# Layer 2's shift as rows on TensorE, layer 1's gate summed through scratch, and a new order from keys to turn

## The chip, the cores and the metric

The kernel runs on one core of a Trainium2 chip. A core has four compute engines with instruction streams of their own: TensorE (PE in the profile, its weight loads PEld), VectorE (DVE), ScalarE (ACT) and GpSimd (POOL); a fifth, SyncE (SP), issues most DMA transfers. The metric is the device time of one execution in microseconds, the median of several. Lower is better.

## What is computed

Two layers of a decoder trunk on 256 tokens of width 1024, then a final RMSNorm. Each layer is modulated by a condition vector `c`:

```python
for i in range(DEPTH):
    shift, scale, gate = jnp.split(c @ ada_w[i] + ada_b[i], 3, axis=-1)
    h = rmsnorm(x, norm_g[i]) * (1.0 + scale[:, None, :]) + shift[:, None, :]
    y = nsa_mixer(h, ...) if i % N_MIXERS == 0 else mlstm_mixer(h, ...)
    x = x + gate[:, None, :] * y
return rmsnorm(x, final_g)
```

Layer 1 (`i = 0`) is a sparse attention with 16 heads in 4 groups and three branches (compressed, selected, sliding), whose outputs are summed with sigmoid gates and multiplied by a SiLU gate path before the output projection. Layer 2 (`i = 1`) is a chunkwise mLSTM with 8 heads. The change concerns layer 1 from its keys on, the passage ("turn") from layer 1 to layer 2's first products, and two parts of the modulation: layer 1's `gate` and layer 2's `shift`, each a vector of 1024 that is a product of `c` (1024) with a 1024 x 1024 block of `ada_w`.

## The kernel before

Tokens lie in two blocks of 128 partitions (index `a`). Every weight product is made in three float32r terms: a weight is rounded on ACT (`hi`, line 164), its rest is taken on DVE (`lo`, line 169), and PE multiplies rounded by rounded, rounded by rest and rest by rounded. Weights come as 512 KB pieces through a ring of ten raw buffers, issued by SP (line 86), and go into rings of six `wh` and six `wl` buffers (`RAW`, `WBUF`).

*First phase* (up to about 54 us). Layer 1's modulation, norm and the products for queries and the first keys, streamed by eight blocks of the width.

*Keys, values and gate logits* (`nsa`, 54 to 71 us). `kv_block(kk)` makes, for each of eight blocks of the width, the remaining keys (`gemm_ws`, lines 1610 to 1612), one branch's values and another's values with the gate logits (`gemm_tok`, lines 539 to 541). The queries' evacuation and the position embedding stand between the blocks, in a loop.

*Attention* (71 to about 155 us). A list written out by hand, `ORDER`, names every step, and since the schedule is manual here each engine runs its instructions in that order. Per head pair `n` (0 to 7): `S` scores, `m` masked minima (DVE), `e` exponentials (ACT, line 780), `f` factors (DVE), a scaling of the probabilities (line 794), `T` transposes on PE (line 799), `t` their copies (ACT, line 624), `V` values (line 816). A scaling has two branches of two instructions; `s` puts both on DVE, `p` both on POOL, `q` one on each. Around them stand `hidden`, `gelu` and the `c...` steps (compressed branch), `z`, `zt`, `zo` (gate path), `y` and `Y` (gated output and its parts), `out` (the output projection, line 869), `hi` and `lo` (weights), and the modulation:

- `d:s,n`, `column` (line 852): layer 2's shift (n = 0, 1) and scale (n = 2, 3). The weights lie with the output on partitions, and one DVE pass over 128 x 1024 multiplies by `c` and sums along the row. Sixteen passes, two blocks of 128 outputs for each `s`.
- `gr`, `gc`, `gs`, `ga`: layer 1's gate as rows. `ada_rows` (line 226) multiplies on PE, four partial sums side by side in four column groups of 32; `gc` copies them to SBUF; `gs` (line 859) is a float32 product with a selector matrix that adds the four rows and spreads the sum to 128 partitions; `ga` (line 863) adds it to the bias, which a broadcast on ACT's queue has put into `gate0`.

*Turn* (about 146 to 192 us). `turn` is a hand-written sequence: the last output blocks (`last`), residual and squares (lines 1067, 1068, 1111), the norm's root, scaling, transposes (1125), modulation (1135 on DVE, 1137 on ACT), rounding (1143, 1145) and rest (1149), and layer 2's first products (1158) of `narrow` (272 wide) and `wide` (512 wide) weights.

*Layer 2* follows under the framework's own scheduler, which orders it by its own estimates.

Of the kernel before, what the change touches and what calls it, by code (L numbers as in the profile page):

```python
# [23 lines left out]
class Kernel:  # L24
# [119 lines left out]
    def make_hi(self, m):  # L144
# [7 lines left out]
        if kind == "z":  # L152
            r4 = raw.rearrange("p k j (i d) -> p k j i d", i=2)
            views = [((lambda w, i=i: w.rearrange("p (k i j d) -> p k i j d", k=4, i=2, j=2)[:, :, i]), r4[:, :, :, i]) for i in range(2)]
        elif kind == "q":
# [95 lines left out]
    def setup(self):  # L251
# [16 lines left out]
        self.ones1 = self.T(self.p1, [P, 1])  # L268
        g.memset(self.ones1, 1.0)
# [13 lines left out]
        self.bif = self.T(pc, [P, 16])  # L283
        self.int1 = self.T(pc, [P, 8], I32)
# [24 lines left out]
    def small_loads(self):  # L309
        nc, t = self.nc, self.t  # L310
        self.first_small = [(self.pca[:, 32:89], t["second"])]
        self.small = [(self.bif, t["gate_b"].partition_broadcast(P)), (self.pcb, t["mixer"]), (self.compress, t["compress"])]


    def layer1(self):
# [30 lines left out]
        for kk in range(KC):  # L346
            self.add("s", [P, 816], t["keys"][kk])
# [167 lines left out]
    def embed(self, n, o):  # L515
# [3 lines left out]
        self.nc.vector.tensor_tensor(F.rearrange("p u g s -> p g s u"), self.E[n][:, :, o : 16 + o], pe.unsqueeze(1).unsqueeze(1).to_broadcast([P, 4, 16, 8]), op=OP.add)  # L519
# [23 lines left out]
    def nsa(self, acc):  # L543
# [30 lines left out]
        def kv_block(kk):  # L574

            wh, wl = self.take()
            first, last = kk == 0, kk == KC - 1
            for ch in range(2):
                sl = slice(256 + ch * P, 256 + ch * P + P)
                self.gemm_ws(bk[:, ch * 256 : ch * 256 + 256], wh[:, sl], wl[:, sl], kk, first=(first and ch == 0), last=last)  # L580
            for a in range(2):
                self.gemm_tok(bv[:, a * 256 : a * 256 + 256], wh[:, 0:256], wl[:, 0:256], kk, a, first=(first and a == 0), last=last)
            for a in range(2):
                self.gemm_tok(bg[a][:, 0:304], wh[:, 512:816], wl[:, 512:816], kk, a, first=first, last=last)


        bk, bg, bv = self.bank(7), [self.bank(4), self.bank(5)], self.bank(6)
        for kk in range(KC):
            kv_block(kk)
            if kk % 2:  # L590
                self.embed(kk // 2 % 2, kk // 4)
            else:
                queries(kk // 2)
            if kk < 6:
                self.split_next()
        self.dup_split((KH, KL), 1, bk)
        for a in range(2):
            nc.scalar.activation(V[1][:, a], bg[a][:, 0:256], AF.Copy)
            nc.scalar.activation(G[:, a], bg[a][:, 256:304], AF.Tanh, scale=0.5)
        nc.vector.tensor_scalar(G, G, 1.0, 0.25, op0=OP.add, op1=OP.mult)  # L600
# [5 lines left out]
    T:0,0,1 m:1,0 gelu:2 p:0,1 params lo z:0,1 e:1,0 turned t:0,0,1 m:1,1 T:0,0,0 t:0,0,0 S:2,0 second e:1,1 T:0,1,1 cvalues:0 T:0,1,0 f:1 t:0,1,0  # L606
    z:0,2 z:0,3 ckeys cscores:0 cscores:1 hi cvalues:1 zt:0 t:0,1,1 m:2,0 q:1,0 S:2,1 ccopy:0 ccopy:1 d:0,1 T:1,0,1 zo:0 ctokens:0 t:1,0,1 m:2,1
    T:1,0,0 p:1,1 cdist:0 ctokens:1 t:1,0,0 cdist:1 z:1,0 e:2,1 z:1,1 bias cexp T:1,1,1 T:1,1,0 lo e:2,0 cprobs f:2 t:1,1,1 cparts:0 z:1,2 cparts:1 t:1,1,0
    S:3,0 z:1,3 S:3,1 zt:1 m:3,0 m:3,1 d:0,2 q:2,0 cturned:0 V:0 V:1 zo:1 e:3,0 p:2,1 cpt:0 T:2,0,0 e:3,1 C:0 f:3 d:0,3 cturned:1 t:2,0,0 s:3,0
    T:2,0,1 d:1,0 T:2,1,0 cpt:1 t:2,1,0 t:2,0,1 hi gr:0 S:4,0 T:2,1,1 y:0 gc:0 m:4,0 gs:0 ga:0 t:2,1,1 T:3,0,0 hi t:3,0,0 p:3,1 lo S:4,1 T:3,0,1 e:4,0  # L610
    t:3,0,1 m:4,1 S:5,0 e:4,1 z:2,0 T:3,1,1 t:3,1,1 T:3,1,0 z:2,1 hi S:5,1 m:5,0 lo f:4 z:2,2 d:1,1 gr:1 m:5,1 p:4,0 t:3,1,0 e:5,1 p:4,1 d:1,2 z:2,3
    hi T:4,0,0 e:5,0 S:6,0 zt:2 V:2 V:3 lo d:1,3 C:1 lo zo:2 t:4,0,0 gc:1 T:4,1,0 t:4,1,0 T:4,0,1 f:5 s:5,0 y:1 t:4,0,1 S:6,1 T:5,0,0 T:4,1,1 d:2,0
    t:5,0,0 m:6,0 p:5,1 t:4,1,1 gs:1 e:6,0 m:6,1 T:5,0,1 t:5,0,1 e:6,1 d:2,1 V:4 d:2,2 S:7,0 f:6 T:5,1,0 p:6,1 z:3,0 T:5,1,1 m:7,0 t:5,1,0 q:6,0 z:3,1
    ga:1 hi S:7,1 T:6,0,0 z:3,2 Y:0 lo hi z:3,3 C:2 m:7,1 t:5,1,1 out:0 V:5 hi lo T:6,0,1 d:2,3 e:7,1 zt:3 d:3,0 e:7,0 t:6,0,0 zo:3 f:7 hi T:6,1,0
    q:7,0 hi out:1 t:6,1,0 t:6,0,1 d:3,1 T:6,1,1 hi lo y:2 Y:1 t:6,1,1 lo root q:7,1 lo V:6 lo Y:2 d:3,2 d:3,3
    """

    def attention(self, hidden_block):
# [171 lines left out]
        def scaled(n, j, *es):  # L790
            for br in range(2):
                for a in range(2):
                    v = probs(n, j, br, a)
                    es[br].tensor_scalar(v, v, F[n][:, a, br, j : j + 1], None, op0=OP.mult)  # L794
# [59 lines left out]
        def gate_bias():  # L854
            nc.scalar.dma_start(self.gate0, t["ada_b"][0:1, 2048:3072].partition_broadcast(P))

        def gate_sum(bank):
            b = B["gs"] = self.bank(bank)
# [836 lines left out]
```

## Time and profile before

| | us |
|---|---|
| median of three runs | 423.44 (423.31 to 423.47) |
| the profiled execution's own time | 423.31 |
| its span, first to last instruction | 421.5 |
| PE busy / DVE busy / ACT busy / POOL busy | 412.3 / 348.6 / 270.8 / 96.6 |

The granted TensorE clock is 0.996 of full speed over the span. A time in the profile counts from the span's start. "Idle before, releaser" in a row is how long the engine stood still before the instruction, and what it waited for last. Matmuls overlap: a record lasts longer than the distance from its start to the next one's, so a stretch in which PE is busy all the time can still hold late starts; the distance between starts shows them.

### The profile page before, as it was taken

To read this page: it belongs to the slowest core of one execution; us is meant where nothing else is said; L and a number is where in the kernel's file an instruction comes from. 1 tells how busy PE (TensorE), PEld (TensorE's weight loads), DVE (VectorE), ACT (ScalarE), POOL (GpSimd) and SP (SyncE) were. 2 spreads that over 40 slices of the span, in tenths; PEclk is the share of its full clock that TensorE was granted. 3 is DMA by queue.
4 is the path that set the end of the run, shared out by engine and by line. 5 is a ranking of instruction groups with operands and counts; after the bars stand their busy time and mean duration, and the time that the engine had idled before them with its cause. 6 is when DMAs were issued, how large, how long until landed. Compare 5 with 4: busy or idle time off the path is not lost.

```text
span 421.5 us, 7600 instructions
## 1 busy us (share of the span) xinstructions
PE 412.3 (98%) x2669; PEld 357.2 (85%) x2669; DVE 348.6 (83%) x736; ACT 270.8 (64%) x541; POOL 96.6 (23%) x154
## 2 busy tenths in 40 slices
PE   8999999999999999999999999999999999999994
PEld 5899999789778877878999999888888888888884
DVE  6999898999999998878592699899858998558554
ACT  6666693788987973668547966565456554565523
POOL 4000112354676750142223200000000240320000
PEclk9999999999999999999999999999999999999998
DMA  8999996963799678239667467467456587640002
GB/s 321 410 407 406 396 322 197 342 274 136 253 334 388 236 251 298 96 119 317 218 226 277 157 193 225 177 205 265 169 176 202 186 296 230 180 143 0 0 2 100
DMA packets 27543, 96.21 MB, mean 228 GB/s; under 512 B 3512, under 2 KB 3616, under 8 KB 27376
## 3 DMA queue, kind: packets, MB, share of 16 engines
q1 hardware_dynamic: 26208, 92.30, 61.9%
q0 software_dynamic: 1008, 2.63, 1.7%
q10 hardware_dynamic: 288, 0.79, 0.5%
q8 instruction: 21, 0.34, 0.3%
q14 instruction: 18, 0.15, 0.1%
HBM read 94.61 MB, written 1.09 MB: 227 GB/s over the span
## 4 chain that ended last, share of the span: by engine, by line
PE 84%; issue 5%; DMA 4%; POOL 2%; DVE 2%; ACT 1%; SPq 0%; DVEq 0%; POOLq 0%
PE bank L539 10%; PE bank L541 10%; PE bank L540 10%; PE bank L433 7%; PE bank L1612 6%; PE bank L1610 6%; PE bank L1611 6%; PE bank L1523 5%; PE bank L1036 5%; PE bank L1158 3%; DMA Q<-in_columns 3%; PE bank L799 2%; PE bank L1403 2%; PE bank L816 2%; PE bank L754 2%
## 5 line engine op out<-in xcount | busy, mean ns | idle before, releaser
L169 DVE TENSOR_TENSOR wl<-raw,wh 128x1024 fp32r<-128x1024 f32 (+4 forms) x127 | 139.3, 1112 | 34.5 <-ACT wh L164 33.8
L164 ACT ACTIVATE wh<-raw 128x1024 fp32r<-128x1024 f32 (+4 forms) x127 | 119.2, 957 | 65.1 <-PE bank L541 28.2
L539 PE MATMUL bank<-wh,one 128*128 128x512 f32 (+1 forms) x208 | 76.9, 370 | 0.0
L540 PE MATMUL bank<-wl,one 128*128 128x512 f32 (+1 forms) x208 | 76.3, 367 | 0.0
L541 PE MATMUL bank<-wh,one 128*128 128x512 f32 (+1 forms) x208 | 76.2, 367 | 0.0
L1610 PE MATMUL bank<-one,wh 128*128 128x256 f32 x208 | 59.6, 287 | 0.0
L1612 PE MATMUL bank<-one,wl 128*128 128x256 f32 x208 | 59.0, 284 | 0.1
L1611 PE MATMUL bank<-one,wh 128*128 128x256 f32 x208 | 58.8, 283 | 0.0
L794 POOL TENSOR_SCALAR Pr<-Pr,f 128x128 f32<-128x128 f32 (+1 forms) x42 | 46.7, 1128 | 32.9 <-DVE f L788 18.8
L539 PEld LDWEIGHTS bank<-wh,one 128*128 128x128 f32 x208 | 39.2, 188 | 6.2 <-DVE tz L511 0.2
L541 PEld LDWEIGHTS bank<-wh,one 128*128 128x128 f32 x208 | 39.2, 188 | 6.2
L540 PEld LDWEIGHTS bank<-wl,one 128*128 128x128 f32 x208 | 39.2, 189 | 6.0
L1610 PEld LDWEIGHTS bank<-one,wh 128*128 128x128 f32 x208 | 39.7, 191 | 1.4 <-issue 0.8
L1612 PEld LDWEIGHTS bank<-one,wl 128*128 128x128 f32 x208 | 39.7, 191 | 0.5 <-DVE wl L169 0.3
L1611 PEld LDWEIGHTS bank<-one,wh 128*128 128x128 f32 x208 | 39.8, 191 | 0.1
L780 ACT ACTIVATE Pr<-Pr,mn 128x128 f32<-128x128 f32 (+1 forms) x64 | 28.2, 444 | 4.3 <-DVE mn L773 4.3
L433 PE MATMUL bank<-one,wh 128*128 128x256 f32 x224 | 29.8, 284 | 0.5 <-ACT one L407 0.4
L433 PEld LDWEIGHTS bank<-one,wh 128*128 128x128 f32 x224 | 28.1, 192 | 0.9 <-ACT one L407 0.6
L160 POOL TENSOR_TENSOR raw<-raw,gate 128x256 f32<-128x256 f32 x16 | 13.6, 858 | 49.7 <-DMA raw<-in_out_b 24.9
L1384 DVE SCALAR_TENSOR_TENSOR conv<-bank,one,conv 128x255 f32<-128x255 f32 (+2 forms) x48 | 20.0, 466 | 2.1 <-ACT conv L1379 2.1
L852 DVE CUSTOM_DVE_ANT_0 raw<-raw,one,one 128x1024 f32<-128x1024 f32 x16 | 21.1, 1330 | 0.0
L773 DVE CUSTOM_DVE_ANT_0 Pr<-bank,one 128x128 f32<-128x128 f32 (+1 forms) x64 | 18.7, 348 | 0.0
(336 smaller groups left out, 793.1 us busy)
## 6 DMA issues: line engine op xcount, KB each, us to landing
raw<-in_wide SPq DMA_DIRECT2D x44, 512.0 KB, 4.4
raw<-in_units SPq DMA_DIRECT2D x18, 512.0 KB, 4.6
raw<-in_turn SPq DMA_DIRECT2D x16, 512.0 KB, 6.8
raw<-in_gates SPq DMA_DIRECT2D x16, 512.0 KB, 4.9
raw<-in_out_b SPq DMA_DIRECT2D x16, 512.0 KB, 3.9
raw<-in_start SPq DMA_DIRECT2D x8, 512.0 KB, 9.7
Q<-in_columns SPq DMA_DIRECT2D x8, 512.0 KB, 9.6
raw<-in_hidden SPq DMA_DIRECT2D x8, 512.0 KB, 4.3
```

Source lines behind the costliest of these rows:

```text
L164: self.nc.scalar.activation(v(hi), src, AF.Copy)
L169: self.nc.vector.tensor_sub(v(lo), src, v(hi).bitcast(F32))
L433: nc.tensor.matmul(out, w[:, ch * P : ch * P + P], h[:, kk], start=(kk == 0 and m == 0 and ch % 2 == 0), stop=(kk == 7 and m == 2), skip_g ...
L539: nc.tensor.matmul(out, self.hh[:, kk, sl], wh, start=first, stop=False, skip_group_check=True)
L540: nc.tensor.matmul(out, self.hh[:, kk, sl], wl, start=False, stop=False, skip_group_check=True)
L541: nc.tensor.matmul(out, self.hl[:, kk, sl], wh, start=False, stop=last, skip_group_check=True)
L780: nc.scalar.activation(v, v, AF.Exp, bias=mn[:, a, br, j : j + 1], scale=-1.0, accum_out=sm[:, a, br, j : j + 1])
L794: es[br].tensor_scalar(v, v, F[n][:, a, br, j : j + 1], None, op0=OP.mult)
L852: nc.vector.tensor_tensor_reduce(raw, raw, self.cbc, scale, self.pca[:, 72 + 8 * b + kc : 73 + 8 * b + kc], OP.mult, OP.add, self.cols1[s] ...
L1610: nc.tensor.matmul(out, wh, self.hh[:, kk], start=first, stop=False, skip_group_check=skip)
L1611: nc.tensor.matmul(out, wh, self.hl[:, kk], start=False, stop=False, skip_group_check=skip)
L1612: nc.tensor.matmul(out, wl, self.hh[:, kk], start=False, stop=last, skip_group_check=skip)
```

## The change

1. Layer 2's shift is made like the gate: `cr` (rows on PE by `ada_rows`, two groups), `cc` (permuted copy on ACT), `c1` (a store of the four partial rows to DRAM scratch by a POOL DMA), `c2` (a load with outputs spread over 128 partitions), `c3` (a transpose of 32 x 32 blocks, a sum over the four parts and the bias, on DVE). The eight `d:s,0` and `d:s,1` passes are gone, and `modulate` takes the shift from `self.shifts`. The weights come as eight pieces of `shift` instead of eight of `turn`.
2. Layer 1's gate is summed through scratch: `g1` stores the four rows, `g2` loads them as 32 partitions, `g3` adds them and the bias (`gbias`) on DVE, `g4` stores the sum, `g5` loads it broadcast to 128 partitions into `gate0`. The selector product and the addition are gone.
3. The keys loop and the turn are taken apart into steps, and `ORDER` is written anew over all of it, from the keys to the turn. Keys have three parts, `k:kk,part`; scalings are `s` with an engine for each branch (`v` DVE, `p` POOL, `a` ACT), so ACT makes some too.
4. The gate path's weights come in the order that PE reads, so that `hi` and `lo` are one instruction for 1024 columns instead of two strided ones for 512.

```diff
-        nc.scalar.activation(V[0].rearrange("p a k -> p (a k)"), bv, AF.Copy)
-        self.attention(hidden)
+        self.attention({"hidden": hidden, "k": kv_block, "qa": queries, "qb": query_rests, "kd": keys_out, "G": gates_out, "vo": values_out,
+                        "E": lambda n, o: self.embed(n, o, nc.vector), "Ea": lambda n, o: self.embed(n, o, nc.scalar)})
...
-    d:0,0 hidden:0 hi hidden:1 S:0,0 lo S:0,1 hi hidden:2 hidden:3 z:0,0 m:0,0 m:0,1 e:0,0 lo S:1,0 e:0,1 f:0 gelu:0 s:0,0 hi S:1,1 gelu:1
...
+    hi k:0,0 k:0,1 hi lo lo k:0,2 k:1,0 k:1,1 E:1,0 k:1,2 k:2,1 E:0,0 k:3,1 k:2,2 k:2,0 hi hi hi lo E:0,1 k:4,1 qa:2 E:1,1 qa:0 k:3,2 hi qa:1 k:3,0
+    k:4,2 lo k:5,2 k:4,0 k:5,1 qa:3 lo qb:3 qb:2 k:5,0 k:6,2 k:6,0 lo k:7,0 qb:1 hi lo hi hi k:7,2 G:0 qb:0 kd lo G:1 hidden:0 vo:1 hidden:1 S:0,0
+    k:6,1 S:0,1 m:0,0 hi e:0,0 hidden:2 vo:0 lo m:0,1 e:0,1 f:0 hidden:3 sap:0,0 S:1,0 k:7,1 gelu:0 m:1,0 gelu:1 vo:2 S:1,1 m:1,1 T:0,0,0 z:0,0
...
+    t:5,1,0 c1:0 T:5,1,1 t:5,1,1 m:7,0 e:7,0 g3 c1:1 g4 hi z:3,2 z:3,3 T:6,1,1 T:6,1,0 m:7,1 e:7,1 lo lo zt:3 out:0 d:3,2 out:1 l:1,1,2 f:7 t:6,1,1
+    svp:7,1 hi spv:7,0 t:6,1,0 T:6,0,1 t:6,0,1 T:6,0,0 lo lo lo g5 hi t:6,0,0 C:2 zo:3 V:5 l:0,0,2 T:7,1,1 l:0,0,3 y:2 lo hi T:7,1,0 l:0,1,2 t:7,1,1
+    t:7,1,0 T:7,0,1 T:7,0,0 t:7,0,0 V:6 lo t:7,0,1 V:7 c2 C:3 l:0,1,3 Y:2 l:0,1,4 l:0,1,5 l:0,0,4 l:0,0,5 nh:1 nl:1 y:3 c3 Y:3 nh:0 l:0,0,6 nl:0 d:3,3
+    l:0,0,7 r:0,0 l:0,1,6 l:0,1,7 l:1,0,2 r:0,1 root sq:0,0 nh:2 sq:0,1 l:1,1,3 l:1,0,3 l:1,1,4 l:1,0,4 nl:2 sc:0 x:0,1 l:1,0,5 l:1,0,6 l:1,0,7 nh:3
+    nl:3 x:0,0 tr:0,0 tr:0,1 nh:4 rp:1,0 md:0,1 l:1,1,5 l:1,1,6 md:0,0 ro:0,0 l:1,1,7 r:1,1 ro:0,1 n:0,0 n:0,1 sq:1,0 v:0,0 sq:1,1 re:0,0 re:0,1 sc:1
+    x:1,1 nh:5 nl:4 v:0,1 n:0,2 v:1,0 v:1,1 x:1,0 tr:1,0 md:1,0 tr:1,1 md:1,1 v:2,0 v:2,1 ro:1,0 ro:1,1 re:1,1 re:1,0 nl:5 v:0,2 v:1,2 n:1,0 n:1,1
+    n:1,2 gt:0 gt:1
...
-        def gate_sum(bank):
-            b = B["gs"] = self.bank(bank)
-            nc.tensor.matmul(b, self.sel, W["A"].pop(0), start=True, stop=True)
-
-        def gate_add(n):
-            g = self.gate0[:, 512 * n : 512 * n + 512]
-            nc.vector.tensor_tensor(g, g, B["gs"], op=OP.add)
+        def four(A):
+            return A.rearrange("(j r) k -> j r k", r=32)[:, 0]
+
+        def gate_store(n):
+            if not n:
+                W["quarters"] = self.pd.tile([4, D], F32, name=self.nm("quarters"), tag="quarters")
+            nc.gpsimd.dma_start(W["quarters"][:, 512 * n : 512 * n + 512], four(W["A"].pop(("gate", n))))
+
+        def gate_load():
+            W["gq"] = T([32, 4, 32])
+            nc.gpsimd.dma_start(W["gq"], W["quarters"].rearrange("j (b c) -> b j c", b=32))
+
+        def gate_sum():
+            W["gv"] = T([32, 32])
+            nc.vector.tensor_reduce(W["gv"], W["gq"].rearrange("b j c -> b c j"), axis=AX.X, op=OP.add)
+            nc.vector.tensor_tensor(W["gv"], W["gv"], self.gbias, op=OP.add)
...
+        def gate_spread():
+            nc.gpsimd.dma_start(self.gate0, W["whole"].rearrange("b c -> (b c)").unsqueeze(0).partition_broadcast(P))
+
+        def shift_store(n):
+            if not n:
+                W["drawer"] = self.pd.tile([4, 2, 16, 32], F32, name=self.nm("shifts"), tag="shifts")
+            nc.gpsimd.dma_start(W["drawer"][:, n].rearrange("q (j k) c -> j q (k c)", j=4), four(W["A"].pop(("shift", n))).rearrange("j (q k) -> j q k", q=4))
+
+        def shift_load():
+            W["sq"], W["st"] = T([P, 32]), T([P, 32])
+            nc.gpsimd.dma_start(W["sq"], W["drawer"].rearrange("q n r c -> (q n r) c"))
+
+        def shift_sum():
+            sh = self.shifts = self.T(pc, [P, 8])
+            nc.vector.transpose(W["st"], W["sq"])
+            nc.vector.tensor_reduce(sh.rearrange("p (n k) -> p n k", n=2), W["st"].rearrange("p (n j k) -> p n k j", n=2, j=4), axis=AX.X, op=OP.add)
+            nc.vector.tensor_tensor(sh, sh, self.pca[:, 72:80], op=OP.add)
```

In the new steps of the turn, `l:a,half,k` is one output block, `r` and `rp` are the residual with its addition on DVE or POOL, `sq` the squares, `sc` the root, `x` the scaling, `tr` the transposes, `md` the modulation, `ro` the rounding, `re` its rest, `n` and `v` the narrow and wide products, `nh` and `nl` the weights' `hi` and `lo`, `gt` the gate logits.

More of the change, by code (lines that the diff above doesn't have):

```diff
@@ L151, in make_hi @@
         kind = self.queue[m][0]
[L152 to L155, printed above, removed]
+        if kind == "q":
             cuts = (slice(0, 2), slice(2, 4)) if m in self.opening else (slice(0, 4),)
@@ L612 @@
[L612 to L615, printed above, removed]
+        kw, banks = [], {}
@@ new lines, in kv_block @@
+        def kv_block(kk, part):
+            while len(kw) <= kk:
+                kw.append(self.take())
+            if not kk:
+                banks[part] = [self.bank(i) for i in ((7,), (6,), (4, 5))[part]]
+            wh, wl = kw[kk]
+            first, last = kk == 0, kk == KC - 1
+            if part == 0:
+                for ch in range(2):
+                    sl = slice(256 + ch * P, 256 + ch * P + P)
+                    self.gemm_ws(banks[0][0][:, ch * 256 : ch * 256 + 256], wh[:, sl], wl[:, sl], kk, first=(first and ch == 0), last=last)
+            elif part == 1:
+                for a in range(2):
+                    self.gemm_tok(banks[1][0][:, a * 256 : a * 256 + 256], wh[:, 0:256], wl[:, 0:256], kk, a, first=(first and a == 0), last=last)
+            else:
+                for a in range(2):
+                    self.gemm_tok(banks[2][a][:, 0:304], wh[:, 512:816], wl[:, 512:816], kk, a, first=first, last=last)
@@ L1107, in square, with narrow_hi, narrow_lo, last @@
+        def narrow_hi(n):
+            half_made[n] = self.make_hi(self.first + n)
+        def narrow_lo(n):
+            self.make_lo(*half_made.pop(n))
+            self._load()
+        def last(a, half, k):
+            while len(held) < k - 1:
+                n = len(held) + 2
+                held[n] = self.take(hold=n > 2)
+            self.out_mm(k, *held[k], a, *self.pieces[a][half])
         def square(a, half):
-            self.residual(p1, self.gate0, a, *pieces[a][half], g=nc.gpsimd if (a, half) in ((1, 0),) else nc.vector)
@@ L1159, in products @@
                                          stop=(k0 + k == KC - 1 and m == 2), skip_group_check=True)
-        held[2] = self.take()
-        for n in range(4):
-            self.step("T", 7, n // 2, n % 2)
-            self.step("t", 7, n // 2, n % 2)
-            if n < 2:
-                self.split_next()
-            last(n % 2, n // 2, [2])
-        for k in range(3, 8):
-            held[k] = self.take(hold=True)
-        hi(2)
-        self.step("V", 7)
-        self.step("C", 3)
-        hi(0)
@@ L1190, in turn @@
-        for half in range(2):
-            last(1, half, [3])
-        for half in range(2):
-            last(1, half, [4, 5])
-        scale(0)
-        hi(3)
-        lo(3)
-        transposed(0)
-        for half in range(2):
-            last(1, half, [6, 7])
-        modulate(0)
-        hi(4)
-        rounded(0)
-        square(1, 0)
-        rest(0, 0)
-        square(1, 1)
-        rest(0, 1)
-        first = [(3 * n, self.take(hold=n > 0)) for n in range(3)]
-        bs = [self.bank(6 + a) for a in range(2)]
@@ L1223, in turn, with narrow @@
-        rest(1, 0)
-        rest(1, 1)
-        lo(5)
-        w.append((4, self.take(hold=True)))
-        products(vs[0], w[2:], 0, 512, (0, 1))
-        products(bs[1][:, 0:272], first, 1, 272)
-        GT = self.T(pc, [P, 2, 16])
-        for a in range(2):
-            nc.vector.tensor_tensor(GT[:, a], bs[a][:, 256:272], self.bif, op=OP.add)
+        def narrow(a, m):
+            if not first:
+                first.extend((3 * n, self.take(hold=n > 0)) for n in range(3))
+            if not m:
+                bs[a] = self.bank(6 + a)
+            products(bs[a][:, 0:272], first, a, 272, (m,))
@@ L1233, in todo, with wide, gates @@
+        def wide(m, n):
+            if not vs:
+                vs.update((a, self.bank(4 + a)) for a in range(2))
+            while len(w) <= n:
+                w.append((2 * len(w), self.take(hold=True)))
+            products(vs[0], w[n : n + 1], 0, 512, (m,))
+        def gates(a):
+            if "t" not in half_made:
+                half_made["t"] = self.T(pc, [P, 2, 16])
+            nc.vector.tensor_tensor(half_made["t"][:, a], bs[a][:, 256:272], self.bif, op=OP.add)
         def todo():
```

281 lines of the change are left out of this document (120 added, 161 removed).

## The prediction

> **What bounds the kernel now.** I read the page's first table first, then the busy time by stretches, then the steps between TensorE's starts.
>
> ```profile
> PE 412.3 (98%) x2669; PEld 357.2 (85%) x2669; DVE 348.6 (83%) x736; ACT 270.8 (64%) x541; POOL 96.6 (23%) x154
> ```
> ```profile
> 72.00:120.00 48.00, 48.00 (x406) 39.21 (x404) 45.44 (x172) 40.28 (x130) 21.94 (x27) 1.00 0.68 256
> 120.00:155.00 35.00, 34.79 (x265) 27.62 (x258) 34.72 (x94) 29.93 (x82) 26.46 (x22) 1.00 0.82 286
> 155.00:192.00 37.00, 36.18 (x194) 29.22 (x193) 31.03 (x57) 22.01 (x40) 7.25 (x22) 1.00 0.56 195
> 192.00:416.00 224.00, 224.00 (x1269) 196.53 (x1268) 171.65 (x307) 130.26 (x211) 29.01 (x41) 1.00 0.54 180
> ```
>
> The columns after the stretch are its length, then busy time of PE, PEld, DVE, ACT and POOL. Two engines look full in the attention (72 to 155 us): PE 82.8 us of 83 and DVE 45.44 + 34.72 = 80.2 us. Which is the bound? A busy PE may be overlap of modelled ends, so I look at where matmuls start. Of a gate-path run in the timeline:
>
> ```profile
> 87.69 0.28 PE L1611 MATMUL bank<-one,wh 128*128 128x256 f32 x1
> ...
> 90.32 0.28 PE L1612 MATMUL bank<-one,wl 128*128 128x256 f32 x1
> ```
>
> Between these two rows lie 22 steps: 2.63 / 22 = 0.120 us from start to start. A record lasts 0.28 us, so each overlaps the next by 0.16. 512-wide products, in a stretch of the chain of waits where PE waits for nothing, step by 6.91 / 30 = 0.23 us, and so they do in the attention:
>
> ```profile
> 350.88 6.91 PE bank L1036 x30
> ```
>
> So TensorE is dense at its own rate, and DVE, though nearly full, keeps up. What TensorE loses to waits from 54 us to 192 us is little:
>
> ```profile
> PE bank L1158 <- DVE one L1145: 0.5, 1, 0.5
> PE bank L816 <- DVE y L825: 0.2, 1, 0.2
> PE bank L1158 <- DVE one L1149: 0.2, 1, 0.2
> ```
>
> Idle after a record's end costs that idle and the lost overlap of 0.16: 0.49 + 0.16 = 0.65, 0.21 + 0.16 = 0.37 and 0.20 + 0.16 = 0.36 us. In the timeline the second one ends here, the third and the first stand with their surroundings:
>
> ```profile
> 149.63 1.52 PE L816 MATMUL bank<-PT,one 128*64 128x256 f32 x16 [0.21 <-DVE y L825]
> ```
> ```profile
> 176.38 1.68 PE L1158 MATMUL bank<-wh,one 128*128 128x272 f32 x8 [0.20 <-DVE one L1149]
> ...
> 178.37 1.04 PE L1125 MATMUL bank<-one,Pr 128*128 128x128 f32 x8
> ...
> 179.44 1.36 DVE L1135 TENSOR_SCALAR tz<-bank,cols 128x128 f32<-128x128 f32 x4 [0.51 <-PE bank L1125]
> ...
> 180.73 0.41 DVE L1145 CAST one<-tz 128x512 fp32r<-128x512 f32 x1
> ...
> 181.29 0.97 PE L1158 MATMUL bank<-wh,one 128*128 128x272 f32 x5 [0.49 <-DVE one L1145]
> ```
>
> After the second token block's transposes (L1125) PE has too few products to cover the modulation (1.36) and the rounding (0.41) on DVE. These three are 1.4 us. Smaller ones, estimated from starts that come 0.1 to 0.3 us late beside their neighbours (at 55, 57.8, 172 and 186 us), make about 1.2 more. So about 2.6 us is all that a better order can win before 192 us, and from 192 to 416 us PE is busy in every microsecond and waits for nothing. The first 54 us and the tail behind 416 us run code that stays.
>
> **The change part by part.** *TensorE.* The shift as rows adds two groups like layer 1's gate rows; summing the gate through scratch removes the two selector products. From the chain of waits:
>
> ```profile
> 107.97 1.85 PE bank L226 x16
> ...
> 110.82 0.98 PE bank L859 x2
> ...
> 119.72 1.85 PE bank L226 x16
> ...
> 129.66 0.86 PE bank L859 x2
> ```
>
> Added 2 x 1.85 = 3.70, removed 0.98 + 0.86 = 1.84, net +1.86 us on the engine that sets the end. Everything else on PE (keys, hidden, scores, turns, gate path, products) is the same work in another order.
>
> *DVE.* It loses half of L852's sixteen column passes, the two gate sums and two of its 22 scalings (the gate path's weight rests, one wide instruction now instead of two strided ones, give back a little more, which I leave out):
>
> ```profile
> L852 DVE CUSTOM_DVE_ANT_0 raw<-raw,one,one 128x1024 f32<-128x1024 f32 x16 | 21.1, 1330 | 0.0
> ...
> L794 DVE TENSOR_SCALAR Pr<-Pr,f 128x256 f32<-128x256 f32 x11 | 4.4, 400 | 0.0
> L794 DVE TENSOR_SCALAR Pr<-Pr,f 128x128 f32<-128x128 f32 x11 | 3.9, 356 | 0.1
> ...
> L863 DVE TENSOR_TENSOR gate<-gate,bank 128x512 f32<-128x512 f32 x2 | 1.4, 676 | 0.0
> ```
>
> 8 x 1.33 + 2 x 0.676 + (0.400 + 0.356) = 12.7 us less. New are five small sums and a turn of at most 128x32. No row has them; they lie between 0.41 (L1145, 128x512) and nothing, and I take 0.3 each, 1.5 us, keeping 0 to 2.1. DVE is freed of some 11.2 us. Since PE does not wait for DVE in 72 to 149 us, this by itself is worth nothing; its worth is that the order can be drawn tighter.
>
> *ACT.* Counted in the new order, 16 scalings come over from POOL and DVE, and two permuted copies of shift rows; the gate path's 16 half-width roundings become 8:
>
> ```profile
> L780 ACT ACTIVATE Pr<-Pr,mn 128x256 f32<-128x256 f32 x32 | 15.8, 498 | 3.2 <-DVE mn L773 3.2
> ...
> L780 ACT ACTIVATE Pr<-Pr,mn 128x128 f32<-128x128 f32 x32 | 12.4, 390 | 1.1 <-DVE mn L773 1.1
> ...
> L164 ACT ACTIVATE wh<-raw 128x512 fp32r<-128x512 f32 x16 | 9.1, 628 | 0.0
> ...
> L164 ACT ACTIVATE wh<-raw 128x1024 fp32r<-128x1024 f32 x8 | 8.3, 1056 | 0.0
> ...
> L624 ACT ACTIVATE adaA<-bank 128x512 f32<-128x512 f32 x2 | 1.2, 587 | 0.1
> ```
>
> 8 x (0.498 + 0.390) + 2 x 0.587 - (16 x 0.628 - 8 x 1.056) = 7.1 + 1.2 - 1.6 = 6.7 us more, against 83 - 40.28 - 29.93 = 12.8 us that ACT idles in the attention. It fits, with 6.1 us over; at nothing, then, and the second rival is what it costs if that cover is gone.
>
> *POOL and scratch.* POOL's scalings go from 42 to 28, and eight DMA issues are put on its queue: two stores, load, store and spread for the gate, two stores and a load for the shift. Nearest rows:
>
> ```profile
> 213.12 1.95 POOL L1353 DMA_DIRECT2D one<-store  x4
> ```
> ```profile
> DT<-shelf POOLq DMA_DIRECT2D x1, 1536.0 KB, 9.7
> ...
> gate<-in_ada_b ACTq DMA_DIRECT2D x1, 512.0 KB, 4.5
> ...
> QK<-drawer POOLq DMA_DIRECT2D x4, 4.0 KB, 4.9
> ```
>
> An issue takes 1.95 / 4 = 0.49 us, together 3.9, less than the 14 scalings gone. The landing counts only where it ends late. The gate's spread (512 KB to 128 partitions) is issued behind POOL's last scalings and must be there at the first residual. In the new order PE has between the two the value products 5, 6 and 7 (L816, 1.52 us each by the row above) and ten output blocks of three 0.23 us products (0.70), 11.6 us, with some turns and two compressed products besides: about 13 us. By the broadcast rows it takes 4.5 (same size) to 9.7 us (three times the size), and POOL, with a last pair of scalings ahead, may be 2 us late: it fits, at nothing. The shift's load is issued right behind it and its sum stands on DVE behind the last gated product, some 9 us on (the three value products, six of the blocks); 4.9 us fits too. Queued behind that sum on DVE are the last head group's rest (L829) and the residuals, so lateness there would reach PE after some 3 us more of products.
>
> *Queues.* SP issues the same bytes: eight 512 KB pieces of shift rows for eight of columns. ACT's queue loses the bias broadcast. Both at nothing.
>
> *Keys.* The key, value and gate-logit products are cut in three parts per block and two are held back as filler between the first scores; the products are the same and steps of 0.12 to 0.14 us go on across parts. Worth only the late start at 57.8 us: 0.2 us gained, between 0 and 0.3.
>
> *Turn.* Followed by hand with the durations quoted, the new order puts four 512-wide pieces (two steps of 0.23 for each of two blocks) behind the second transposes instead of three, and every rest in time. The 0.36 at 176 us goes, of the 0.65 at 180 us about 0.55 goes; the start at 172 us stays, since there are only three output blocks (2.1 us) ahead where there were four. The wait at 149.6 us goes as values 7 stand right behind values 6. Together 0.36 + 0.55 + 0.37 = 1.3; with the keys 1.5 us.
>
> **Sum**: +1.86 - 1.5 = +0.36; for new waits in the attention I leave nothing, between -0.5 (small late starts vanish) and +1.1 (eleven more of 0.1 us). On the profiled execution's 423.31 us (span 421.5 and 1.8 around it) that is 423.67, and the median before, 423.44, lies 0.13 above that execution. I say **423.6**, with its own range 422.8 to 424.8: no change by what a measurement here can tell (0.2%, 0.85 us).
>
> **The rivals.** *All waits go* (faster): 2.6 us won against 1.86 paid, and the small gaps at switches halved, another 0.5: 423.31 + 1.86 - 3.1 = 422.1 us. For it: DVE's 11.2 us of freed time lies where every one of those waits comes from. Against it: the waits at 55 and 186 us come from code that stays.
>
> *ACT becomes the late engine* (slower). Its idle time is mostly waits that come with the chain itself:
>
> ```profile
> ACT PT L624 <- PE bank L799: 4.5, 6, 1.7
> ACT Pr L780 <- DVE mn L773: 4.3, 5, 1.5
> ```
>
> If these 8.8 us stay, ACT needs 70.2 + 6.7 + 8.8 = 85.7 us in a stage of 83, and its turned copies (L624) hold the banks that PE turns into: 2.7 us late, 426.3; half of it, 425.0. It decides where more than 6.1 us of them remain. DVE being freer speaks against it, as nearly half of them wait for DVE.
>
> *A round trip ends late* (slower): 9.7 us for the spread and 4.9 for the shift's load behind it on the same queue are 14.6 us where 9 are covered up to DVE's sum and 3 more by products behind it: 2.6 us late, 426.2. Landings of more than 12 us together decide it; the 4.5 of the same-size broadcast speaks against.
>
> *DVE is the bound after all* (faster). Then 11.2 us less on DVE would shorten the stage by as much: 423.31 - 11.2 = 412.1 us. The quoted steps of 0.12 us speak against it, and PE's waits for DVE of 0.9 us in all. The Trainium skill (Perfetto Trace Analysis, Identifying the Most-Contended Engine) holds matmul busy time for a bad measure and would judge TensorE's headroom by its weight loads. By that rule PE has room here, as PEld is busy 39.21 of 48 us, and DVE with 45.44 is the most contended engine; the starts in the trace show no such room.
>
> That the shift's rows do not do what they say (columns still made) would show as sixteen L852 passes; the order has eight such steps, so I give it nothing.
>
> **How the numbers follow.** Forecast 0.60, all waits go 0.17, ACT late 0.14, round trip late 0.06, DVE the bound 0.03. Faster by over 0.2% (below 422.6): the two faster rivals, 0.20. Slower by over 0.2% (above 424.3): the two slower ones and the top of the forecast's own range, 0.14 + 0.06 + 0.05 = 0.25. Same: 0.55. The range 422.0 to 425.2 takes in the forecast with its bounds, the first rival and ACT's up to a half.
>
> **What would show it.** Right: 64 records of L226's kind with 128x512 where there were 32 and none of the selector products; steps of 0.12 and 0.23 us as now; DVE busy some 11 us less; PE's waits on DVE at the second rounding near 0.1 us. Wrong: PE waiting for ACT's turned copies or scalings (second rival), for the first residual's gate or a DVE sum behind a DMA (third), or a stage from 72 to 155 us that has shrunk by more than 3 us (fourth).

## The result, and the profile after

The changed kernel takes 428.25 us (427.98 to 428.67, four runs) against 423.46 us (423.31 to 424.23, four runs) for the kernel before on the same chip: ratio 1.0112, 95% interval 1.0097 to 1.0127. It is 1.1% slower. The forecast was 423.6 us, and the time lies above the range of 422.0 to 425.2.

The first table of the page after, and the busy time by the same stretches as before (length, then busy time of PE, PEld, DVE, ACT and POOL):

```profile
PE 416.2 (98%) x2697; PEld 359.1 (84%) x2697; DVE 336.9 (79%) x713; ACT 276.1 (65%) x551; POOL 85.0 (20%) x148
```
```profile
72.00:120.00 48.00, 47.21 (x405) 38.58 (x402) 37.71 (x143) 39.78 (x131) 14.01 (x20) 1.00 0.63 225
120.00:155.00 35.00, 34.23 (x263) 27.05 (x263) 31.11 (x98) 27.93 (x80) 18.82 (x22) 1.00 0.86 337
155.00:192.00 37.00, 36.92 (x215) 30.45 (x215) 29.68 (x58) 23.66 (x44) 6.32 (x21) 1.00 0.53 174
192.00:416.00 224.00, 224.00 (x1240) 194.01 (x1239) 169.99 (x300) 130.69 (x209) 33.55 (x44) 1.00 0.55 180
```

DVE lost 11.7 us of busy time and ACT gained 5.3, about as counted (11.2 and 6.7). In the attention PE now has small holes (47.21 of 48 us and 34.23 of 35, where it was 48.00 and 34.79), in the turn fewer (36.92 of 37, where it was 36.18). The last row is the surprise: from 192 to 416 us PE is busy all the time, as before, but gets through 1240 products instead of 1269. A part of that is only the later start of this stretch, so the next cut is made at products and not at times.

Where along the span did the time come? I took the starts of three products that both kernels have: the last of the first phase, the last of the turn (the rows of lines 1158 before and 1192 after), and the last one of all (line 1523 before, 1510 after). Of the kernel before:

```profile
L1158 PE MATMUL bank<-wl,one x32: 284/340/482, 173.6 to 192.0; 128*128 128x272 f32 x16, 128*128 128x512 f32 x16
```
```profile
415.76 0.28 PE L1523 MATMUL bank<-late,V 128*128 128x256 f32 x1
```

and of the changed one:

```profile
L1192 PE MATMUL bank<-wl,one x32: 284/342/480, 176.2 to 193.8; 128*128 128x272 f32 x16, 128*128 128x512 f32 x16
```
```profile
420.37 0.28 PE L1510 MATMUL bank<-late,V 128*128 128x256 f32 x1
```

| stretch of TensorE | before | after | difference | predicted |
|---|---|---|---|---|
| up to the last first-phase product | 52.26 | 52.57 | +0.31 | 0 |
| from there to the last product of the turn | 139.79 | 141.24 | +1.45 | +0.36 |
| from there to the last product | 223.72 | 226.55 | +2.83 | 0 |

The largest part lies in a stretch whose code did not change, in which both kernels run 1268 products and PE waits for nothing. So the products themselves must be slower. The source rows of the second of `gemm_tok`'s three products (`tok_unit` calls it all through layer 2), 208 records, before (line 540) and after (541), with the shortest, median and longest duration in ns:

```profile
L540 PE MATMUL bank<-wl,one x208: 280/389/400, 53.2 to 392.4; 128*128 128x512 f32 x80, 128*128 128x256 f32 x16, 128*128 128x304 f32 x8
```
```profile
L541 PE MATMUL bank<-wl,one x208: 277/395/401, 53.5 to 397.0; 128*128 128x512 f32 x80, 128*128 128x256 f32 x16, 128*128 128x304 f32 x8
```

The same products last 395 ns instead of 389. Start to start, in the timeline near 200 us, before:

```profile
199.75 0.39 PE L540 MATMUL bank<-wl,one 128*128 128x512 f32 x1
...
202.69 0.39 PE L541 MATMUL bank<-wh,one 128*128 128x512 f32 x1
```

and after:

```profile
199.44 0.39 PE L540 MATMUL bank<-wh,one 128*128 128x512 f32 x1
...
204.82 0.39 PE L542 MATMUL bank<-wh,one 128*128 128x512 f32 x1
```

Before, 13 steps in 2.94 us are 0.226 each; after, 23 steps in 5.38 us are 0.234. Over the 480-odd 512-wide products of this kind the mean rose from 227.9 to 234.1 ns: 480 x 6.2 ns = 3.0 us, enough for the whole of the +2.83. The granted clock is 1.00 in this stretch in both.

In the middle stretch the waits changed places. PE's waits after, from the view of waits:

```profile
PE bank L776 <- POOL KL L534: 0.8, 1, 0.8
PE bank L821 <- POOL Pr L816: 0.8, 2, 0.6
```

Gone are the waits for DVE that ended at 149.6, 176.4 and 181.3 us (of the last a late start of 0.17 us is left) and two smaller late starts at 57.8 and 172.5 us. New are two for POOL. The timeline of POOL shows what it did before the second one:

```profile
115.72 0.57 POOL L884 DMA_DIRECT2D quarters<-adaA  x1 [1.83 <-ACT adaA L643]
121.12 0.58 POOL L888 DMA_DIRECT2D one<-quarters  x1 [4.83 <-DVE wl L166]
121.74 4.62 POOL L816 TENSOR_SCALAR Pr<-Pr,f 128x128 f32<-128x128 f32 x6
```

`g2`, the load of the four quarters, reads what `g1` has just stored. It stood 4.83 us at the head of POOL's queue, and the scalings of head pair 3 stood behind it. The releaser that the row names (a `wl` on DVE) has nothing to do with this load; the store's landing fits, and a later run names it.

### The profile page after: what moved, and what is told of

It is laid out like the page before. It is cut to its first block, busy times and chain, and to the rows that moved or that the text cites. A ratio compares the mean times of both kernels' runs of the same rounds, so it can differ in the third digit from the quotient of the medians.

```text
span 426.2 us, 7639 instructions
## 1 busy us (share of the span) xinstructions
PE 416.2 (98%) x2697; PEld 359.1 (84%) x2697; DVE 336.9 (79%) x713; ACT 276.1 (65%) x551; POOL 85.0 (20%) x148
## 4 chain that ended last, share of the span: by engine, by line
PE 86%; DVE 4%; DMA 3%; ACT 2%; issue 1%; SPq 1%; POOL 1%; DVEq 0%; ACTq 0%
PE bank L541 9%; PE bank L542 9%; PE bank L540 9%; PE bank L430 8%; PE bank L921 5%; PE bank L1510 5%; PE bank L1081 5%; PE bank L1597 5%; PE bank L1599 5%; PE bank L1598 5%; PE bank L1192 4%; PE bank L838 3%; DMA raw<-in_start 2%; PE bank L821 2%; PE bank L1390 2%; PE bank L773 2%
## 5 line engine op out<-in xcount | busy, mean ns | idle before, releaser
L540 PE MATMUL bank<-wh,one 128*128 128x512 f32 (+2 forms) x208 | 77.9, 375 | 0.0
L541 PE MATMUL bank<-wl,one 128*128 128x512 f32 (+2 forms) x208 | 77.3, 372 | 0.0
L542 PE MATMUL bank<-wh,one 128*128 128x512 f32 (+2 forms) x208 | 77.1, 372 | 0.0
L1598 PEld LDWEIGHTS bank<-one,wh 128*128 128x128 f32 x208 | 39.4, 189 | 0.1
L1597 PEld LDWEIGHTS bank<-one,wh 128*128 128x128 f32 x208 | 39.1, 188 | 0.1
L816 POOL TENSOR_SCALAR Pr<-Pr,f 128x128 f32<-128x128 f32 (+1 forms) x28 | 25.5, 925 | 24.6 <-DVE f L807 15.3
L430 PEld LDWEIGHTS bank<-one,wh 128*128 128x128 f32 x224 | 28.0, 189 | 1.1 <-ACT one L404 0.6
L157 POOL TENSOR_TENSOR raw<-raw,gate 128x256 f32<-128x256 f32 x16 | 16.3, 1028 | 48.2 <-DMA raw<-in_out_b 24.6
L643 ACT ACTIVATE PT<-bank 128x384 f32<-128x384 f32 x32 | 14.9, 486 | 8.3 <-PE bank L821 8.3
```

The costliest lines, as they stand in the source:

```text
L430: nc.tensor.matmul(out, w[:, ch * P : ch * P + P], h[:, kk], start=(kk == 0 and m == 0 and ch % 2 == 0), stop=(kk == 7 and m == 2), skip_g ...
L540: nc.tensor.matmul(out, self.hh[:, kk, sl], wh, start=first, stop=False, skip_group_check=True)
L541: nc.tensor.matmul(out, self.hh[:, kk, sl], wl, start=False, stop=False, skip_group_check=True)
L542: nc.tensor.matmul(out, self.hl[:, kk, sl], wh, start=False, stop=last, skip_group_check=True)
L816: es[br].tensor_scalar(v, v, f, None, op0=OP.mult)
L1597: nc.tensor.matmul(out, wh, self.hh[:, kk], start=first, stop=False, skip_group_check=skip)
```

## The experiments

Two theories. **Placement**: two small tiles of the change (`gbias`, 128 bytes a partition, and `shifts`, 32) lie ahead of the weight rings in SBUF (the on-chip memory that holds all tiles, each at its address in the partitions) and push them on by 160 bytes, while `hh` and `hl`, the other operand of these products, stay; dense products are slower for it. **Queue**: the new waits of the attention come from steps that POOL or DVE holds at the head of its queue for a landing. The rival to the first is that the new order or its traffic (scratch, streams) slows layer 2.

**1. a_home**: the changed kernel, its order untouched, with the two tiles where they do not move the rings.

```diff
-        self.gbias = self.T(pc, [32, 32])
+        self.gbias = self.T(self.p1, [32, 32])
+        self.shifts = self.T(self.p1, [P, 8])
...
-            sh = self.shifts = self.T(pc, [P, 8])
+            sh = self.shifts
```

> The changed kernel with its two new small tiles (gate bias, 128 bytes per partition, and shifts, 32) taken from the layer 1 pool instead of the constant pool; every instruction and its order stay. The weight rings then begin at byte 41088 as before (0 modulo 64) and not at 41248 (32 modulo 64). Theory 'place of the rings': the 480 products of 512 columns in layer 2 that stream weights against the norm's rows step by 0.227 to 0.230 us again instead of 0.234 to 0.236; layer 2 gets 2.9 us back; time 425.3. Rival 'layer 2's neighbours' (another order or another timing of DVE, ACT and DMA beside the products): the steps stay at 0.234 and the time at 428.2.

Measured: 425.28 us (424.3 to 425.76, ten runs) against 423.96, ratio 1.0027, interval 1.0017 to 1.0038. Its source row of the same product:

```profile
L542 PE MATMUL bank<-wl,one x208: 278/389/400, 53.2 to 393.3; 128*128 128x512 f32 x80, 128*128 128x256 f32 x16, 128*128 128x304 f32 x8
```

389 ns again, and 223.70 us from the turn to the end, as before. Placement is shown, and three quarters of the loss with it (1.12% to 0.27%).

**2 and 3. b_pad32, b_pad64**: the kernel before with an unused tile ahead of the rings.

```diff
         self.bif = self.T(pc, [P, 16])
+        self.T(pc, [P, 8])        # b_pad32; [P, 16] in b_pad64
```

> The kernel before with 32 unused bytes per partition in the constant pool, so that the weight rings begin at 32 modulo 64; nothing else. Place of the rings: 512-wide steps of 0.234 us in layer 2, 426.3 us. Layer 2's neighbours: 423.4, since no instruction moves.

> The kernel before with 64 unused bytes: the rings keep 0 modulo 64 and move by 64 modulo 128. If the place counts modulo 64: steps of 0.227 to 0.230 us and 423.4. If it counts modulo 128 or more: steps up to 0.234 us and up to 426.3. Layer 2's neighbours: 423.4.

Measured: with 32 bytes 425.38 us (424.89 to 426.37) against 423.96, ratio 1.0036, interval 1.0026 to 1.0046; the 512-wide step is 233.2 ns. So an unused tile alone, with no change of code, slows the kernel by half as much as was expected. Half, because the 256-wide products, whose stationary operand is the weight, became faster at the same time: 119.7 to 118.2 ns. With 64 bytes the single run gave 422.24 us, less than the kernel before: 512-wide 229.6, but 256-wide 116.5 ns. Of this gain 0.89 us was there at the end of the first phase already (51.37 us against 52.26 in the trace of the kernel before), and from the turn to the end it takes 223.65 us, hardly less than before. A rule by the place within 64 bytes gives neither the 229.6 nor the 116.5.

**4. b_gate**: the kernel before with only the gate through scratch, its steps at the places of the old ones and its bias tile in layer 1's pool, where it does not move the rings. Two of the changed lines of `ORDER`:

```diff
-    T:2,0,1 d:1,0 T:2,1,0 cpt:1 t:2,1,0 t:2,0,1 hi gr:0 S:4,0 T:2,1,1 y:0 gc:0 m:4,0 gs:0 ga:0 t:2,1,1 T:3,0,0 hi t:3,0,0 p:3,1 lo S:4,1 T:3,0,1 e:4,0
+    T:2,0,1 d:1,0 T:2,1,0 cpt:1 t:2,1,0 t:2,0,1 hi gr:0 S:4,0 T:2,1,1 y:0 gc:0 m:4,0 g1:0 t:2,1,1 T:3,0,0 hi t:3,0,0 p:3,1 lo S:4,1 T:3,0,1 e:4,0
...
-    ga:1 hi S:7,1 T:6,0,0 z:3,2 Y:0 lo hi z:3,3 C:2 m:7,1 t:5,1,1 out:0 V:5 hi lo T:6,0,1 d:2,3 e:7,1 zt:3 d:3,0 e:7,0 t:6,0,0 zo:3 f:7 hi T:6,1,0
+    g3 g4 hi S:7,1 T:6,0,0 z:3,2 Y:0 lo hi z:3,3 C:2 m:7,1 t:5,1,1 out:0 V:5 hi lo T:6,0,1 d:2,3 e:7,1 zt:3 d:3,0 e:7,0 t:6,0,0 zo:3 f:7 hi T:6,1,0
```

> The kernel before with one part of the change alone: layer 1's gate summed through scratch (two stores, load, sum with the bias on DVE, store, spread), put into the old order at the places of the old steps, the spread behind POOL's last scaling. Rings at their old place. If TensorE's work sets the time, the two selector products (0.98 + 0.86 us) go and nothing comes: 421.6. If a round trip ends late, PE waits before the first residual or a DVE sum: 423.4 or more.

Measured: 428.33 us (428.16 to 428.67), ratio 1.0100, interval 1.0083 to 1.0116. The expectation of 421.6 was missed by 6.7 us, though the two selector products are gone. The timeline of DVE shows one of the two places, that of POOL the other:

```profile
142.46 0.36 DVE L866 TENSOR_REDUCE one<-adaA 32x32 f32<-32x128 f32 x1 [4.45 <-DMA adaA<-quarters]
```
```profile
111.22 0.62 POOL L858 DMA_DIRECT2D quarters<-adaA  x1 [4.11 <-PE bank L800]
111.89 4.00 POOL L795 TENSOR_SCALAR Pr<-Pr,f 128x128 f32<-128x128 f32 x4
```

The sum `g3` held DVE for 4.45 us until the load had landed; a `lo` stood behind it, and PE waited 2.7 us for that. And the first store held POOL until the rows were copied, so that head pair 3's scalings began at 111.89 us. (The store's row names PE as releaser; the copy that it reads stands in ACT's timeline and ended at 110.93 us.)

```profile
110.33 0.60 ACT L625 ACTIVATE adaA<-bank 128x512 f32<-128x512 f32 x1
```

In the kernel before POOL's timeline has the scalings here:

```profile
107.52 4.92 POOL L794 TENSOR_SCALAR Pr<-Pr,f 128x128 f32<-128x128 f32 x4 [0.72 <-DVE f L788]
```

They came 4.4 us late, and PE's transposes of them cost 1.3 us. A step that takes 0.4 us by itself costs what stands behind it.

PE's wait had a second cost. Its row in the timeline, and the view by stretches right behind it, where the column ahead of the last two is the granted clock:

```profile
144.83 0.79 PE L880 MATMUL bank<-wl,Q 128*128 128x512 f32 x1 [2.67 <-DVE wl L169]
```
```profile
144.60:147.90 3.30, 3.07 (x7) 2.42 (x8) 3.30 (x11) 2.75 (x10) 0.00 (x0) 0.50 0.51 159
```

During the wait the granted clock fell to 0.50 and stayed there until about 148 us. The seven 512-wide steps from 144.83 us on took 3.15 us together, where 0.23 each would be 1.6: about 1.5 us more. In start times the wait for DVE is 2.8 us, the slow clock 1.5, the two late transposes 1.3 and a wait for a copy on ACT 0.9; less the selectors' 1.84 that is 4.7 us, against 4.44 measured from the first phase to the end of the turn.

**5. a_two**: a_home with two steps moved: `g2` behind the scalings that it held up, and one part of the key products ahead of the first scores, for the wait at 74 us (POOL was still copying the second half of `KL`).

```diff
-    k:7,2 G:0 qb:0 kd lo G:1 hidden:0 vo:1 hidden:1 S:0,0
-    k:6,1 S:0,1
+    k:7,2 G:0 qb:0 kd lo G:1 hidden:0 vo:1 hidden:1 k:6,1 S:0,0
+    S:0,1
...
-    T:3,0,0 g2 d:1,2
+    T:3,0,0 d:1,2
...
-    sva:4,0 spa:3,1 T:3,1,0
+    sva:4,0 spa:3,1 g2 T:3,1,0
```

> The changed kernel with the two tiles back home, and with two steps of the order moved: the scratch load of the gate's quarters stands behind the scalings of head group 3 on POOL instead of ahead of them, and one part of the key products (block 6, values) stands ahead of the first scores instead of behind. Theory (the new waits are queue waits: POOL holds the load until the store before it has landed, 4.73 us, with those scalings behind it; the first scores come before POOL has copied the second half of KL): both PE waits go, 0.88 and 0.60 us of idle and the lost overlap, 0.95 + 1.15 = 2.1 us in all; 425.3 - 2.1 = 423.2 us on the scale of the run before, ratio to the kernel before about 0.998. Rival (POOL is simply late with its work, or the next step on PE is late by as much): the waits move to the next consumers and the time stays at 424.8 to 425.4 us.

Measured: 422.90 us (422.65 to 423.16, five runs) against 423.76, ratio 0.9971, interval 0.9956 to 0.9985. The timeline of POOL:

```profile
115.49 1.54 POOL L817 TENSOR_SCALAR Pr<-Pr,f 128x128 f32<-128x128 f32 x2
120.84 0.62 POOL L889 DMA_DIRECT2D one<-quarters  x1 [3.81 <-DMA quarters<-adaA]
```

The load still waits, and now its row names the store's landing, but nothing that PE needs stands behind it. In the busy times by stretches PE has no hole left there:

```profile
120.00:155.00 35.00, 35.00 (x273) 27.94 (x273) 31.94 (x99) 27.92 (x79) 17.64 (x20) 1.00 0.91 348
```

The middle stretch is 138.97 us where a_home's was 140.73: 1.76 us for two moved steps (2.1 expected; 0.2 us of the first wait stays).

**6. a_two64**: a_two with the rings 64 bytes further on, as in b_pad64.

```diff
-        self.shifts = self.T(self.p1, [P, 8])
+        self.shifts = self.T(pc, [P, 16])[:, 0:8]
...
-            W["gq"] = T([32, 4, 32])
+            W["gq"] = T([P, 128], tag="gq")[0:32].rearrange("b (j c) -> b j c", j=4)
...
-            W["sq"], W["st"] = T([P, 32]), T([P, 32])
+            W["sq"], W["st"] = T([P, 32]), T([P, 128], tag="gq")[:, 0:32]
```

The last two lines only make room: the shift's turned copy takes the buffer of the gate's quarters, used long before.

> The same order as in the run above (a_two), and the rings 64 bytes further on in memory (the shift tile takes 64 instead of 32 bytes ahead of them). Theory (steps depend on where the operands lie, to a grain finer than 128 bytes, as in the kernel before with 64 bytes: 256-wide steps 120.0 to 116, 512-wide steps 227.8 to 229.5): about 600 steps of 256 columns that PE makes densely shorten by 3 ns and 480 of 512 grow by 1.7 ns, net 1.0 to 1.2 us less: 422.1 us on the scale of a_two's 423.2. Rival (the single run of the kernel before with 64 bytes was chance, or belongs to that order): the same time as a_two within 0.4 us.

Measured: 420.91 us (420.6 to 421.51, four runs) against 423.76, ratio 0.9923, interval 0.9906 to 0.9941. 1.99 us below a_two, more than the 1.0 to 1.2 expected, and 1.5 of it from the turn to the end: the 256-wide step fell to 115.4 ns, the 512-wide one rose to 229.5. The same place in memory did more in this order than in the old one, and why is open. This is the fastest kernel of the study, faster than both.

**7 and 8. b_all32 and b_hh32**: does the moving operand's place count, or its distance from the stationary one? In b_all32 everything moves by 32 bytes, in b_hh32 only `hh` and `hl` do.

```diff
+        self.T(pc, [P, 8])                      # b_all32
+        self.eps = self.T(pc, [P, 1])           # b_hh32, moved here from behind hl
         self.hh = self.T(pc, [P, KC, SEQ], F32R)
         self.hl = self.T(pc, [P, KC, SEQ], F32R)
```

> The kernel before with an unused tile of 32 bytes ahead of hh, so that hh and hl (stationary) and the rings (moving) all lie 32 bytes further on. Theory 1 (what counts is how the moving operand lies against the stationary one, as layer 2's query and key products suggest, whose operands moved together and kept 231 us x 1000 steps): tok_unit's 512-wide steps stay at 228 ns, and the time within 0.7 us of the kernel before. Theory 2 (what counts is the moving operand's own place within 64 bytes): 234 ns, and some 1.5 to 2.9 us more.

> The kernel before with the tile of the epsilon put ahead of hh: hh and hl lie 32 bytes further on, the rings where they were. Theory (what counts is the distance between the two operands): tok_unit's 512-wide steps, now with the moving operand 32 bytes short of where it was against the stationary one, rise from 228 to 231 to 234 ns, 1.5 to 3 us more. Rival (the moving operand's own place decides): they stay at 228 ns, since the rings have not moved.

Measured: b_all32 424.24 us, 512-wide step 228.0 ns, 223.72 us from the turn to the end: as before. b_hh32 424.13 us (before: 424.06), 512-wide step 233.1 ns, 224.93 us. The source rows of b_all32 (line 541) and of b_hh32 (540):

```profile
L541 PE MATMUL bank<-wl,one x208: 280/389/400, 54.1 to 393.3; 128*128 128x512 f32 x80, 128*128 128x256 f32 x16, 128*128 128x304 f32 x8
```
```profile
L540 PE MATMUL bank<-wl,one x208: 277/395/397, 52.7 to 393.1; 128*128 128x512 f32 x80, 128*128 128x256 f32 x16, 128*128 128x304 f32 x8
```

389 ns where both operands moved, 395 where only the stationary one did and the moving one stayed. So neither operand's own place decides, but the distance between the two. b_hh32's whole time stays near that of before because its 256-wide products went to 116.8 ns and its start was 0.5 us earlier at the end of the first phase.

**9 and 10. b_pad128 and b_pad192**: is there a period? The edit is that of b_pad32 with `[P, 32]` and `[P, 48]`.

> The kernel before with 128 unused bytes ahead of the rings. If only the place within 64 bytes counts, everything is as before (512-wide 228 ns, 256-wide 120 ns; same time). If 64 bytes gave b_pad64 its 117 ns and 229.5 ns by the distance itself, 128 gives other steps again: 256-wide below 120 ns, or 512-wide above 229 ns.

> The same with 192 bytes. If the pattern repeats at 128 bytes, this is b_pad64 again: 256-wide 116 to 117 ns, 512-wide 229.5 ns, about 1.2 us less than before. If it repeats at 64, nothing changes against the kernel before. If the distance counts over a longer stretch, neither.

Measured: 425.62 and 424.71 us (before: 424.06). No period of 64 or 128 bytes. All places together, by what the distance from `hh` to the rings differs from the kernel before; steps are means from start to start, some 490 and 930 of them in each trace, the last column goes from the turn's last product to the last of all:

| bytes | kernel | 512-wide, ns | 256-wide, ns | us |
|---|---|---|---|---|
| 0 | before | 227.9 | 119.7 | 223.72 |
| 0 | b_all32 (both moved) | 228.0 | 119.7 | 223.72 |
| 0 | a_home | 227.9 | 119.8 | 223.70 |
| -32 | b_hh32 | 233.1 | 116.8 | 224.93 |
| +32 | b_pad32 | 233.2 | 118.2 | 225.49 |
| +64 | b_pad64 | 229.6 | 116.5 | 223.65 |
| +64 | a_two64 | 229.5 | 115.4 | 222.18 |
| +128 | b_pad128 | 232.6 | 118.9 | 225.64 |
| +160 | the changed kernel | 234.1 | 119.9 | 226.55 |
| +192 | b_pad192 | 233.3 | 117.8 | 225.40 |

The kernel before's distance has the fastest 512-wide steps of all, the changed one's the slowest of both kinds. That single traces are good enough for this shows at distance 0: all seven traces with it (also a_two, b_gate, b_gate2 and b_gate2_again, five orders in all) have 223.70 to 223.72 us in the last column. The last column follows the steps; whole times of single runs do not as closely, since the end of the first phase alone wandered from 51.4 to 53.1 us over these kernels.

**11 and 12. b_gate2, b_gate2_again**: b_gate with its scratch steps where nothing stands behind them.

```diff
-    t:4,1,1 g1:1 g2 e:6,0
+    t:4,1,1 e:6,0
...
-    f:6 T:5,1,0 p:6,1 z:3,0
+    f:6 T:5,1,0 g1:1 p:6,1 g2 z:3,0
...
-    g3 g4 hi S:7,1
+    hi S:7,1
...
-    lo root q:7,1 g5 lo V:6
+    lo root g3 q:7,1 g4 g5 lo V:6
```

(`g1:0` likewise goes behind `p:3,1`.)

> The kernel before with only the gate through scratch, as in b_gate, but with the five scratch steps moved to where nothing that PE needs stands behind them: the first store behind group 3's scalings on POOL, the second store ahead of and the load behind group 6's, the sum on DVE late, just ahead of the last group's scalings, the way out behind those. Theory (b_gate's 4.4 us were two queue waits: group 3's scalings 4.4 us late behind the first store, and DVE idle for 4.45 us at the sum until the load has landed; the two selector products are worth 1.84 us as predicted): 424.0 - 1.84 = 422.1 us, from 421.9 to 422.9. Rival (the round trip cannot be covered in the old order, and the residuals wait for the gate): 424 us or more, with PE waiting behind the first residual.

> b_gate2 once more, for a trace of its other time: its ten runs lay at 422.9 to 423.4 us (three) and at 427.5 to 428.6 us (seven), and the trace of b_gate2 is of a run of the first kind. Theory 1 (a landing through scratch comes late in those runs, and the queue behind it): the trace shows one wait of 4 to 5 us on TensorE, behind the residuals or a group's turned scores, ahead of 192 us. Theory 2 (the chip gives the kernel a lower clock in such runs): the dense steps of 0.120 and 0.228 us are some 1.2% longer everywhere and no wait is new.

Measured: ten runs of b_gate2 gave 422.88, 423.15, 423.38 and seven times 427.5 to 428.6 us (median 427.74, ratio 1.0069, interval 1.0037 to 1.0101, which mixes the two); one more gave 423.64. Both traces are of the lower kind. In them neither of b_gate's two long waits is left, and b_gate2's middle stretch takes 139.36 us, 0.43 less than before. The selectors' 1.84 us are not won in full: the second one had covered a copy on ACT, for which PE now waits.

```profile
PE bank L800 <- ACT PT L625: 0.7, 1, 0.7
```

What makes this kernel 5 us slower in most of its runs is not settled, as no trace caught one; I do not count it for either theory. The mean granted clock gives a hint: it is 0.993 or 0.994 in six of the seven long runs, as in b_gate's runs (0.994 and 0.995), and 0.997 or 0.998 in the three short ones; no other run in this study is under 0.996. A stretch at half clock like b_gate's, 3.4 of 427 us, takes 0.004. So a long wait of PE with such a stretch behind it fits six of them; the seventh (428.55 us) has 0.999 and does not fit. A clock lower by 1.2% throughout, the other theory of b_gate2_again, fits none. a_two and a_two64 showed no such runs in five and four.

## Why the prediction was wrong

- **The bound**: right. TensorE set the end at its start-to-start steps. The rival by which DVE is the bound fell: DVE's busy time sank by 11.7 us and the time rose; even in a_two the middle stretch is only 0.82 us shorter than before. The rule of the Trainium skill (Perfetto Trace Analysis, Identifying the Most-Contended Engine), taken by the weight loads alone as I weighed it there, would have led astray in this kernel.
- **The step that failed**: "from 192 to 416 us PE is busy in every microsecond and waits for nothing" was read as if it said that this stretch costs the same after the change. The sum has no term for it, so it stood at nothing, without a reason. The code there stays, its tiles do not: from the turn to the end it cost 2.83 of the 4.7 us of span, by 6 ns on each 512-wide product, and a_home takes it back. I read the two new allocations in the diff as space and never asked what lies behind them.
- **New waits in the attention** ("nothing", bounds -0.5 to +1.1): wrong, 1.76 us by a_two. The queue part said that POOL's eight issues take 0.49 us each (0.6 measured) and that SP and ACT lose or keep theirs. It did not name what stands behind a load that waits for the store before it: 4.83 us with head pair 3's scalings behind it. The landing was looked for only at its reader, where it was covered, as predicted.
- **TensorE's own work** (+1.86): 64 records of the rows step by 7.14 us together where 32 took 3.71, so +3.43 instead of 3.70; with the selectors' 1.84 gone +1.59.
- **Waits won** (-1.5): better than predicted. a_two's middle stretch is 0.82 us shorter than before in spite of the 1.59 us of work, so 2.4 us of waits and late starts are gone (reckoned from what is left, not counted one by one), near the 2.6 of the rival "all waits go". The late start at 172 us, which was to stay, went too.
- **ACT** (6.7 us more, hidden): right, 5.3 us and no wait of PE for it in the attention. The round trips were covered at their readers.

The middle stretch adds up: 1.59 - 2.4 + 1.76, and about 0.5 us for placement there (141.24 against a_home's 140.73), is the +1.45 of the table. Without the two faults the change is what a_two shows, 0.3% faster than before, and a shift of the rings by 64 bytes, which no view of the profile before suggested, gives more than the new order does (0.9971 to 0.9923).

## What to carry to other kernels

When a change allocates, look at which tiles move, and compare the same dense instructions in both traces from start to start before looking for a wait: a busy engine may be slower per instruction. A DMA that reads back what another has just stored can hold the engine that issues it (3.8 and 4.8 us here); put it behind what others need, and the same for a sum behind a load. Behind a long wait of TensorE look at the granted clock too: in b_gate a wait of 2.7 us cost another 1.5. Work removed from the bound engine is worth its time only where it was not the cover of another wait.

## What was not expected of the hardware

A dense float32r product of 512 columns took 227.9 to 234.1 ns from start to start, depending on how far apart in the partition its moving and its stationary operand lie, in steps of 32 bytes and with no period up to 192. One of 256 columns took 115.4 to 119.9 with the same changes, but not by the distance alone (116.5 and 115.4 at +64 bytes in two orders); the two widths do not go together. Moving both operands left the steps as they were. The Trainium skill (SBUF — State Buffer, Operand start alignment) tells where an operand may start and says that its runs timed nothing; every place tried here is a legal start. What in the memory makes the difference, these runs do not show.

In b_gate the granted clock fell to 0.50 while TensorE waited for 2.7 us, and stayed there for 3.4 us; 512-wide steps took 0.427 us in it. From 10 to 413 us no other trace here has such a fall, and none has a wait of TensorE over 1.01 us. How long a wait has to be, these runs do not show.
